# Loads of a streaming mean-subtraction kernel moved from SyncE to GpSimd, with the single-packet flag

## The chip, the cores and the metric

The kernel runs on one core of a Trainium2 chip. The metric is the device time of one execution in microseconds (us); a kernel is compared with the kernel before in alternating rounds on the same chip. Executions agree with their median within 0.3% or better (the widest range here is 1333.54 to 1338.91 us about 1336.73), and all the runs told here were in the fast state, with a granted clock of 1.0.

Some words. HBM is the chip's main memory, SBUF a core's memory on the chip, of which a tile here takes 128 partitions (rows). Sixteen DMA engines, by the profile page's count, move data between the two. A descriptor is one piece of such a transfer, here a partition's row of 33,792 B unless a run cuts it; the trace lists each as one of its "packets" (8192 of them are the 276.8 MB of the loads). The packet that the flag asks for, meant here as a group of descriptors, is not seen in the trace. Landing is the time from the issue of a transfer until its last part is reported as done. SyncE, GpSimd and the scalar engine issue transfers, each on a queue of its own (q1, q0 and q10 in the profiles); the vector engine (DVE) computes.

## The reference

```
x: (8, 4096, 2112) float32
x_r = x.reshape(B, S // 4, 4, D)
pooled = x_r.mean(axis=2)
return x - np.repeat(pooled, 4, axis=1)
```

Groups of four sequence positions lose their mean. 276.8 MB are read and as many written; nothing is used twice.

## The kernel before

A tile is 128 groups, one per partition, each with its four rows of 2112 floats side by side (33,792 B, contiguous in HBM as well). 64 tiles pass through six buffers. Cuts are marked.

```
xg = x.rearrange("b (g f) d -> (b g) (f d)", f=STRIDE)
...
io_pool = ctx.enter_context(tc.tile_pool(name="io", bufs=IO_BUFS))     # IO_BUFS = 6
sum_pool = ctx.enter_context(tc.tile_pool(name="sum", bufs=1))
for g0 in range(0, G, P):
    x_tile = io_pool.tile([P, W], mybir.dt.float32)                    # W = 4 * 2112
    nc.sync.dma_start(out=x_tile[:gsz], in_=xg[g0:g0 + gsz])           # L39: load
    ...
    # L43, L45: three adds into s;  L46: x_tile = s * (-1/4) + x_tile
    ...
    nc.scalar.dma_start(out=og[g0:g0 + gsz], in_=x_tile[:gsz])         # L54: store
```

Of the kernel before, what the change touches and what calls it, by code (L numbers as in the profile page):

```python
# [1 line left out]

# [4 lines left out]

STRIDE = 4
IO_BUFS = 6  # L10


@with_exitstack
def kernel(
    ctx: ExitStack,
    tc: tile.TileContext,
    x: bass.AP,
    out: bass.AP,
):



    nc = tc.nc
    B, S, D = x.shape
    P = nc.NUM_PARTITIONS
    assert S % STRIDE == 0
    G = (B * S) // STRIDE
    W = STRIDE * D

    xg = x.rearrange("b (g f) d -> (b g) (f d)", f=STRIDE)  # L30
    og = out.rearrange("b (g f) d -> (b g) (f d)", f=STRIDE)

    io_pool = ctx.enter_context(tc.tile_pool(name="io", bufs=IO_BUFS))
    sum_pool = ctx.enter_context(tc.tile_pool(name="sum", bufs=1))

    for g0 in range(0, G, P):
        gsz = min(P, G - g0)
        x_tile = io_pool.tile([P, W], mybir.dt.float32)
        nc.sync.dma_start(out=x_tile[:gsz], in_=xg[g0:g0 + gsz])  # L39

        rows = x_tile[:gsz].rearrange("p (f d) -> p f d", f=STRIDE)
        s = sum_pool.tile([P, D], mybir.dt.float32)
        nc.vector.tensor_add(out=s[:gsz], in0=rows[:, 0, :], in1=rows[:, 1, :])  # L43
        for f in range(2, STRIDE):
            nc.vector.tensor_add(out=s[:gsz], in0=s[:gsz], in1=rows[:, f, :])  # L45
        nc.vector.scalar_tensor_tensor(  # L46
            out=rows,
            in0=s[:gsz, None, :].to_broadcast([gsz, STRIDE, D]),
            scalar=-1.0 / STRIDE,
            in1=rows,  # L50
            op0=mybir.AluOpType.mult,
            op1=mybir.AluOpType.add,
        )
        nc.scalar.dma_start(out=og[g0:g0 + gsz], in_=x_tile[:gsz])  # L54


# [1 line left out]
_INS = ['x']  # L58
_OUTS = [((8, 4096, 2112), 'float32')]


# [23 lines left out]
```

## Time and profile before

| | before |
|---|---|
| median time | 1286.48 us (3 runs, 1286.46 to 1286.77) |
| span in the profile | 1284.7 us |
| vector engine (DVE) busy | 1026.1 us, 80% |
| DMA engines in loads / stores | 50.0% / 49.9% of 16 engines' span |
| load / store, issue to landing | 59.6 / 43.8 us (median) |

The prediction shows the lines and reads them.

### The profile page before, as it was taken

Reading aid. Unit: us, or ns where it says so; the run is one execution under the profiler, and the core shown is the slowest. Engines: PE = TensorE matmul, PEld = TensorE weight load, DVE = VectorE, ACT = ScalarE, POOL = GpSimd, SP = SyncE. Lnnn points to the kernel's source line nnn. Section 1 sums busy time; section 2 is a strip of 40 time slices with the busy share of each in tenths; the row PEclk is TensorE's granted clock in tenths of the full one; section 3 lists DMA queues with packets and bytes.
Section 4 is the critical chain, followed back from the end, with each engine's and each line's share of the span. In section 5 each row is a group of like instructions: output and inputs, shape, how many; then the busy total and the mean of one; then the engine's idle time right before and its main releaser. Section 6 shows DMA issues by size and latency. Waiting matters only on the chain.

```text
span 1284.7 us, 674 instructions
## 1 busy us (share of the span) xinstructions
DVE 1026.1 (80%) x256; POOL 0.2 (0%) x4
## 2 busy tenths in 40 slices
DVE  5998778787787877878778787787887878778784
POOL 0000000000000000000000000000000000000000
DMA  9999999999999999999999999999999999999998
GB/s 404 421 438 438 433 425 437 438 427 432 437 437 426 435 437 431 429 437 437 431 428 438 437 431 429 437 436 432 428 438 436 430 430 437 437 426 433 438 431 380
DMA packets 18437, 553.70 MB, mean 431 GB/s; under 512 B 2048, under 2 KB 2048, under 8 KB 2048
## 3 DMA queue, kind: packets, MB, share of 16 engines
q1 hardware_dynamic: 9216, 276.83, 50.0%
q10 hardware_dynamic: 9216, 276.83, 49.9%
q14 instruction: 5, 0.04, 0.0%
HBM read 276.82 MB, written 276.82 MB: 431 GB/s over the span
## 4 chain that ended last, share of the span: by engine, by line
DVE 80%; another core or an unknown queue 17%; DMA 1%; issue 1%; DVEq 0%
DVE x_tile L46 45%; DVE s L45 24%; DVE s L43 12%; DMA x_tile<-in_x_dram 1%; DVEq L43 0%
## 5 line engine op out<-in xcount | busy, mean ns | idle before, releaser
L46 DVE SCALAR_TENSOR_TENSOR x_tile<-s,x_tile 128x8448 f32<-128x8448 f32 x64 | 573.3, 8958 | 2.2
L43 DVE TENSOR_TENSOR s<-x_tile 128x2112 f32<-128x2112 f32 x64 | 150.9, 2358 | 237.5 <-DMA x_tile<-in_x_dram 237.3
L45 DVE TENSOR_TENSOR s<-s,x_tile 128x2112 f32<-128x2112 f32 x128 | 301.8, 2358 | 4.4
L69 POOL MEMSET const-bfloat16-1.0<- 128x1 bf16 x1 | 0.1, 103 | 0.0
L69 POOL MEMSET const-uint8-127<- 128x1 uint8 x1 | 0.1, 102 | 0.0
L69 POOL MEMSET const-float32-0.0<- 128x1 f32 x1 | 0.1, 100 | 0.2 <-issue 0.2
L69 POOL MEMSET const-float32-1.0<- 128x1 f32 x1 | 0.1, 99 | 0.0
## 6 DMA issues: line engine op xcount, KB each, us to landing
x_tile<-in_x_dram SPq DMA_DIRECT2D x64, 4224.0 KB, 59.6
out_dram<-x_tile ACTq DMA_DIRECT2D x64, 4224.0 KB, 43.8
```

Source lines behind the costliest of these rows:

```text
L43: nc.vector.tensor_add(out=s[:gsz], in0=rows[:, 0, :], in1=rows[:, 1, :])
L45: nc.vector.tensor_add(out=s[:gsz], in0=s[:gsz], in1=rows[:, f, :])
L46: nc.vector.scalar_tensor_tensor(out=rows, in0=s[:gsz, None, :].to_broadcast([gsz, STRIDE, D]), scalar=-1.0 / STRIDE, in1=rows, op0=mybir. ...
L69: nc = _bacc.Bacc("TRN2", target_bir_lowering=False, num_devices=1)
```

## The change

The intent is to take loads off the SyncE queue, issue them from GpSimd (the trace calls its queue software_dynamic), and ask by the flag for one packet with an engine's whole share of a tile (8 rows and one small packet of the trace, 9 descriptors: 9216 in a queue, over 64 tiles and 16 engines).

```
-        nc.sync.dma_start(out=x_tile[:gsz], in_=xg[g0:g0 + gsz])
+        nc.gpsimd.dma_start(out=x_tile[:gsz], in_=xg[g0:g0 + gsz], single_packet=True)
```

## The prediction

> **What bounds the kernel now.** The kernel streams 64 tiles of 128 rows by 33,792 bytes (four sequence positions of 2112 floats) from HBM to SBUF, works on them with the vector engine and streams them back. I read first the busy shares and the slices of the span, then the DMA queues:
>
> ```profile
> DVE 1026.1 (80%) x256; POOL 0.2 (0%) x4
> ...
> DMA  9999999999999999999999999999999999999998
> GB/s 404 421 438 438 433 425 437 438 427 432 437 437 426 435 437 431 429 437 437 431 428 438 437 431 429 437 436 432 428 438 436 430 430 437 437 426 433 438 431 380
> DMA packets 18437, 553.70 MB, mean 431 GB/s; under 512 B 2048, under 2 KB 2048, under 8 KB 2048
> ...
> q1 hardware_dynamic: 9216, 276.83, 50.0%
> q10 hardware_dynamic: 9216, 276.83, 49.9%
> ```
>
> The DMA row is 9 (90% or more) in all slices but the last, and the two queues together hold 99.9% of the time of the 16 DMA engines: 50.0% for the loads, 49.9% for the stores. Nothing is left to fill. The vector engine has 20% to spare. The same in one size: 9216 packets of a queue over 64 DMAs and 16 engines are 9 for each engine and DMA, that is 8 rows and one small packet (the 2048 under 512 B)[...]. 50.0% of 16 x 1284.7 us over 8192 data packets is 1.255 us for a packet of 33,792 B, 26.9 GB/s for an engine. 16 engines times this are 431 GB/s, the measured mean.
>
> Next, what the waits say, by groups and by DMA issue:
>
> ```profile
> L46 DVE SCALAR_TENSOR_TENSOR x_tile<-s,x_tile 128x8448 f32<-128x8448 f32 x64 | 573.3, 8958 | 2.2
> L43 DVE TENSOR_TENSOR s<-x_tile 128x2112 f32<-128x2112 f32 x64 | 150.9, 2358 | 237.5 <-DMA x_tile<-in_x_dram 237.3
> L45 DVE TENSOR_TENSOR s<-s,x_tile 128x2112 f32<-128x2112 f32 x128 | 301.8, 2358 | 4.4
> ...
> x_tile<-in_x_dram SPq DMA_DIRECT2D x64, 4224.0 KB, 59.6
> out_dram<-x_tile ACTq DMA_DIRECT2D x64, 4224.0 KB, 43.8
> ```
>
> One tile costs the vector engine 3 x 2.358 + 8.958 = 16.03 us, and it then waits about 237.3 / 59 = 4.0 us for the next load: a period of 20.0 us, which is what 2 x 8 packets of 1.255 us take on each DMA engine. The chain of waits puts 80% on the vector engine, but that is only because it follows the compute in preference to queues; it must not be read as a vector-bound kernel, since every round of it holds a wait of 4 us that a transfer ends.
>
> The buffers close the account. A buffer is 59.6 us in a load (issue to landing), 16.0 in the vector engine and 43.8 in a store: 119.4 us, six times 19.9. So of six buffers about 3 wait in the load queue, 0.8 is being worked on, 2.2 wait in the store queue. The DMA engines always have both kinds of work queued. The wait of the queue that issues the loads says the same from the other side:
>
> ```profile
> SPq L39 <- DMA out_dram<-x_tile: 1158.5, 58, 40.6
> SPq L39 <- DMA x_tile<-in_x_dram: 9.9, 1, 9.9
> ```
>
> Each load from the seventh on is released by the store that frees its buffer, 1158.5 / 58 = 20.0 us apart.
>
> [...] From the trace, (8958 - 2358) ns over (8448 - 2112) elements is 1.042 ns per element, or 0.96 elements per ns[...]. No run yet shows GpSimd beside it. [...]
>
> **The change part by part.** *Removed:* 64 load issues on SyncE, 0.33 us each, off the path. *Added:* 64 issues on GpSimd[...]. [...] even 2 us each would be 64 x 2 = 128 us of an engine that is busy 0.2 us of 1285. Their delay matters only if the DMA engines have nothing else to do meanwhile. They have: see the count of buffers. On the path lies only the first load[...]. *Kept:* bytes, rows, tile, six buffers, the order on the vector engine and the stores. The order of instructions shows one more thing: the loads now have completion semaphores of their own, so the first six are issued at once (before, the sixth waited 9.9 us for the first load to land), and each later one waits for the store that frees its buffer, as before. The sixth load sits behind five others in the queue either way: 0 us.
>
> *Moved:* the share of the engines. Before, an engine did one load row, one store row, in turn. [...] With the load landed 13 us after its buffer came free and 16 us of compute after that, the buffer joins the store queue at 29 us and has 120 - 29 = 91 us to wait and go out: store issue to landing should rise from 43.8 to about 90 us. The period must stay 20 us, because each engine still moves 16 rows of 1.255 us per tile. The buffers that queued for loads queue for stores; this moves a wait, it does not remove one.
>
> [...]
>
> *Start and end.* 64 x 16 rows x 1.255 = 1285 us is the whole span already; idle at both ends is about 2 us. At the end, loads that run early let the vector engine finish well before the stores do, so the last tens of us should be stores alone at full rate; before, the last store took 13.6 us against 10.0 of pure transfer, after the vector engine had ended. That is worth 0 to 2 us[...].
>
> Sum: 1286.5 + 1.5 (start) - 1 (end) - 1 (packets, mostly not believed) = 1286.
>
> **The rivals.** *A: software descriptors starve.* If the vector instructions lock GpSimd out, an issue waits up to 9 us for the 8.96 us instruction. [...] Even if so, the load would land after 22 us in place of 13, in a cycle of 120: the store queue still holds four tiles, 40 us of work, and the time stays. Conversely GpSimd may hold the vector engine up; with 4 us to spare in every 20, up to 4 us per tile is free. Time: 1286 to 1290. *B: the long packet[...] slow the transfer,* or one engine of the 16. As nothing is spare, this comes through in full: 3% on the loads alone is 1.5% or 19 us, 5% is 32 us and beyond the 2% mark. For: saturated engines, a path unmeasured here. Against: 9 descriptors for 270 KB in each engine are next to nothing, and load-only traffic at the start already runs at 439 GB/s from 13 to 29 us. *C: loads ahead of stores are a gain.* The vector engine's wait of 4.0 us per tile looks like a prize of 237 us. It is not: the wait follows from the transfer period, and a load landing earlier only lets its store queue earlier. [...] *D: stores starve until all six buffers await stores or compute and the engines run dry of loads.* Then they do stores, which is work that has to be done too; the engines idle only if all six buffers await the vector engine, which needs 16 us against 20. Time: unchanged.
>
> **Range and chances.** The sum gives 1286. Below, 4 to 5 us by packets and end: 1281. Above, a start of some us more or a rate lower by 0.3%: 1292. Faster by over 2% would need 440 GB/s and more[...]: 0.01. Slower by over 2% is rival B at 5% of the loads, or a serious stall that the buffers do not hide: 0.06. Within 2%: 0.93.
>
> **What the profile after would show.** Right: DMA row still 9 throughout, 431 GB/s, a load queue of software kind at about half the engines' time, vector waits of about 4 us per tile on loads, load to landing 12 to 14 us, stores about 90 us. If the landings stay at 59.6 and 43.8, packets do not set the turns as I hold. If the load queue's share of the engines rises well over 50% for the same bytes, it is rival B, and the prediction fails by half that rise. If 1285 us of DMA time stretches with slices below 9, the engines ran dry (A or D). [...]

The sum came to 1286 us; its three terms are printed, and the end (-1) rests on early loads: all three, and the 4 to 5 us that the range allows below, are guesses. The 12 to 14 us to landing held that with the flag an engine works through a load's eight rows before it turns to a store. This was an assumption that no trace had shown. The turns before the change are in the trace: from 600 us on, in stretches of 1.25 us, 11 rows of one queue start beside 5 or 6 of the other, and in the next stretch the reverse. Against rival A the trace had only the 1.042 ns an element; what that means for GpSimd was not shown yet.

## The result, and the profile after

The changed kernel took 1287.53 us in the median (5 runs, 1287.30 to 1287.59), beside 1286.77 us for the kernel before (5 runs, 1286.46 to 1286.93). The ratio is 1.0006, with a 95% interval of 0.9992 to 1.002: the same. Ratios here are the mean time of one kernel's fast runs over that of the other's fast runs of the same rounds, so they are not quite the ratio of the medians quoted. The ranges of the two kernels do not overlap, so 0.8 us may well be real, but it is 0.06%.

The page of the changed kernel, busy shares, slices and DMA queues:

```profile
DVE 1026.1 (80%) x256; POOL 34.2 (3%) x68
...
DMA  9999999999999999999999999999999999999998
...
q0 software_dynamic: 9216, 276.83, 50.0%
q10 hardware_dynamic: 9216, 276.83, 49.9%
```

The queue of the loads is now of software kind. It has the same 9216 packets and the same half of the engines' time. As before, 50.0% of 16 x 1285.8 us over 8192 data packets is 1.256 us a row: a row is neither quicker nor slower (the median row of the trace takes 1.251 us in both kernels).

The groups with waits, and the DMA issues, of the same page:

```profile
L43 DVE TENSOR_TENSOR s<-x_tile 128x2112 f32<-128x2112 f32 x64 | 151.0, 2359 | 238.4 <-DMA x_tile<-in_x_dram 238.2
L39 POOL DMA_DIRECT2D x_tile<-in_x_dram x64 | 34.0, 532 | 1161.9 <-DMA out_dram<-x_tile 1161.1
...
x_tile<-in_x_dram POOLq DMA_DIRECT2D x64, 4224.0 KB, 59.1
out_dram<-x_tile ACTq DMA_DIRECT2D x64, 4224.0 KB, 43.8
```

Three readings. GpSimd spends 532 ns on an issue, 34 us in all. The 58 issues after the first six all began and ended inside a vector instruction (56 in an add, two in the 8.96 us instruction) and took 530 ns like the others. The vector engine's wait for loads is 238.2 us, against 237.3 before. And the last two lines contradict the prediction: it expected loads to land in 12 to 14 us and stores in about 90, and they stand where they stood.

So the engines do not drain a load's eight rows in one go. The trace names no engine, but the DMA queues show this if one asks for stretches as short as one row. These are the queue lines of the changed kernel from 600 to 601.25 us, and then from 601.25 to 602.5 us (packets that start there, MB, share of 16 engines):

```profile
q0 software_dynamic: 15, 0.51, 93.8%
q10 hardware_dynamic: 1, 0.03, 6.3%
```
```profile
q10 hardware_dynamic: 15, 0.51, 93.8%
q0 software_dynamic: 1, 0.03, 6.3%
```

In one row's time 15 of the 16 engines start a load row, in the next 15 start a store row; the two stretches after repeat this. With turns of a whole load, load rows would have filled eight such stretches in a row. With this flag set, the engines change queues after every descriptor of 33,792 B. An assignment of the packets to engines by start and end finds the same in the whole middle of the run (190 to 990 us): all but two of 5117 load turns are one row long.

Where do the 0.8 us come from? The timeline from the start, first of the kernel before, then of the changed one (start, duration, engine, line, operation, and in brackets the idle time before):

```profile
0.73 12.64 SPq L39 DMA_DIRECT2D x_tile<-in_x_dram  x6
13.05 2.36 DVE L43 TENSOR_TENSOR s<-x_tile 128x2112 f32<-128x2112 f32 x1 [13.05 <-DMA x_tile<-in_x_dram]
```
```profile
1.25 3.27 POOL L39 DMA_DIRECT2D x_tile<-in_x_dram  x6 [0.81 <-PEq L80]
13.89 2.36 DVE L43 TENSOR_TENSOR s<-x_tile 128x2112 f32<-128x2112 f32 x1 [13.89 <-DMA x_tile<-in_x_dram]
```

SyncE issued its first load at 0.73 us, GpSimd at 1.25. The first load then takes 12.32 us to reach the vector engine from SyncE, 12.64 from GpSimd. Together this is 0.84 us. The last vector instruction starts 0.93 us later than before (1262.23 against 1261.30) and the span is 1.1 us longer, so the start travels through to the end of a pipeline without slack. What counts is when the DMA engines begin, not the vector engine: the first data packet of the trace starts at 1.74 us before and at 2.62 us after, and the last one ends 0.95 us later (1284.51 against 1283.56 us). Two runs below start the vector engine some 7 and 12 us later than the changed kernel and lose far less than that.

### The profile page after: what moved, and what is told of

It reads as the page before. It is cut to its first block, busy times and chain, and to the rows that moved or that the text cites. A ratio compares the mean times of both kernels' runs of the same rounds, so it can differ in the third digit from the quotient of the medians.

```text
span 1285.8 us, 676 instructions
## 1 busy us (share of the span) xinstructions
DVE 1026.1 (80%) x256; POOL 34.2 (3%) x68
## 3 DMA queue, kind: packets, MB, share of 16 engines
q0 software_dynamic: 9216, 276.83, 50.0%
q10 hardware_dynamic: 9216, 276.83, 49.9%
## 4 chain that ended last, share of the span: by engine, by line
DVE 80%; another core or an unknown queue 17%; DMA 1%; issue 1%; DVEq 0%; PEldq 0%
DVE x_tile L46 45%; DVE s L45 24%; DVE s L43 12%; DMA x_tile<-in_x_dram 1%; DVEq L43 0%; PEldq L80 0%
## 5 line engine op out<-in xcount | busy, mean ns | idle before, releaser
L46 DVE SCALAR_TENSOR_TENSOR x_tile<-s,x_tile 128x8448 f32<-128x8448 f32 x64 | 573.3, 8958 | 2.2
L43 DVE TENSOR_TENSOR s<-x_tile 128x2112 f32<-128x2112 f32 x64 | 151.0, 2359 | 238.4 <-DMA x_tile<-in_x_dram 238.2
L39 POOL DMA_DIRECT2D x_tile<-in_x_dram x64 | 34.0, 532 | 1161.9 <-DMA out_dram<-x_tile 1161.1
## 6 DMA issues: line engine op xcount, KB each, us to landing
x_tile<-in_x_dram POOLq DMA_DIRECT2D x64, 4224.0 KB, 59.1
out_dram<-x_tile ACTq DMA_DIRECT2D x64, 4224.0 KB, 43.8
```

What stands on the lines that cost most here:

```text
L39: nc.gpsimd.dma_start(out=x_tile[:gsz], in_=xg[g0:g0 + gsz], single_packet=True)
L43: nc.vector.tensor_add(out=s[:gsz], in0=rows[:, 0, :], in1=rows[:, 1, :])
L46: nc.vector.scalar_tensor_tensor(out=rows, in0=s[:gsz, None, :].to_broadcast([gsz, STRIDE, D]), scalar=-1.0 / STRIDE, in1=rows, op0=mybir. ...
```

## The experiments

The questions are these. Does the flag do anything, and what sets the engines' turns (theory D: every descriptor; rivals: the packet, or bytes)? The letters B, C, D, G and P in the expectations are explained there and are not the prediction's rivals of the same letter; A and A' go back to its rival A. Does giving loads a larger share gain anything? Is the start the cost? Would a GpSimd that is held up have been hidden? Each run gives its median beside the median of the kernel before on the same chip.

**The flag alone.**

```
-        nc.gpsimd.dma_start(out=x_tile[:gsz], in_=xg[g0:g0 + gsz], single_packet=True)
+        nc.gpsimd.dma_start(out=x_tile[:gsz], in_=xg[g0:g0 + gsz])
```

> The changed kernel without the single-packet flag, loads still from GpSimd. Theory D (an engine changes queue after every descriptor, so the flag cannot move shares): landings stay near 59.1 us for loads and 43.8 us for stores, 1251 ns per row packet, time 1287.5 within 0.5 us. Rival P (the flag does set the turn, but something else holds the landings): landings or GpSimd's 532 ns per issue change visibly. Rival C (the flag costs or saves time that offsets the start): the time moves by 1 us or more.

1287.46 us beside 1286.54 (ratio 1.0007, 0.9994 to 1.0021), landings 59.1 and 43.8 us, 532 ns an issue. Without the flag the kernel is the same in every number within the noise: no effect of the flag is seen here, and the 0.8 us belong to the move to GpSimd. (The first vector instruction came at 14.05 us here and at 13.89 with the flag, with the issue at 1.25 us in both: the start is known to some 0.2 us.)

**Loads in small descriptors, with the flag and without.**

```
-                            single_packet=True)
+                            single_packet=True, max_dma_last_dim=5632)
```

> Changed kernel with each load row cut in six descriptors of 5632 B[...]; stores keep 33792 B. Theory D (turn after each descriptor): while both queues have work a load gets 5632 of 39424 bytes, 1/7, so stores rush: store landing about 13 to 16 us, load landing about 120 - 16 - 15 = 89 us. Rival P (turn after the packet of 48): loads rush, landing 12 to 15 us, stores near 90. Rival B (turns by bytes): 59 and 44 stay. Time in all: 1287.5 if a descriptor costs nothing of its own[...].

1319.65 us beside 1286.54 (ratio 1.0256, 1.0242 to 1.027). The DMA issues of this run:

```profile
x_tile<-in_x_dram POOLq DMA_DIRECT2D x64, 4224.0 KB, 89.1
out_dram<-x_tile ACTq DMA_DIRECT2D x64, 4224.0 KB, 16.0
```

A load now hands the engine over after 5632 B and a store after 33,792 B, so stores overtake. The order of the packets shows the turns themselves: by the same assignment to engines, a store row is followed by one small load piece in 4316 of 4961 cases in the middle of the run; the rest are mostly long runs of load pieces (22 to 82), which fits a store queue that is empty once a store has landed (16.0 us of a period of 20). Theory D said 89 and 13 to 16; turns by packet would have given the reverse, turns by bytes no change. The time rose by 33 us. The load queue now has 51.0% of 1317.8 us for an engine, 672 us, in place of 50.0% of 1285.8, 643 us: 29 us for 5 x 512 more descriptors in an engine. (A piece takes 0.218 us, six of them 1.31 us, in place of 1.251 for a row.) The end costs too, since the stores no longer have a queue to work on while the last tiles load and are computed. The windows of the end:

```profile
1290.00:1300.00 10.00, 9.90 (x4) 0.00 (x0) 1.00 0.60 260
1300.00:1310.00 10.00, 5.51 (x1) 0.00 (x0) 1.00 0.38 162
```

The last two columns are DMA share and GB/s: some 10 us of idle engines in 20. The two terms add up to more than the 32 us by which the spans differ, because the packets' times in the trace overlap by some 8 us an engine more than in the changed kernel.

> Loads from GpSimd in six descriptors a row, without the single-packet flag. With it the run of small loads measured 89.1 us and 16.0 us to landing and 1319.65 us. Theory D (turns by descriptor, flag of no effect on turns): the same landings within 1 us, time 1317 to 1322. Rival (packets do play a part with several descriptors in a default packet, or the flag saves descriptor cost): landings or time move by more than that.

The same without `single_packet=True`: 1318.79 us (1318.31 to 1319.11) beside 1286.54, in place of 1319.65 (1317.24 to 1321.26).

```profile
x_tile<-in_x_dram POOLq DMA_DIRECT2D x64, 4224.0 KB, 89.0
out_dram<-x_tile ACTq DMA_DIRECT2D x64, 4224.0 KB, 16.0
```

Even with 49 descriptors in an engine's share, the flag changes neither turns nor time.

> The same small descriptors, loads from SyncE. Theory D: the turn is taken by descriptor on the hardware path as well, landings near 89 and 16 us, and the cost of 6 times as many descriptors is again about 33 us over 1286.5. Rival[...]: time clearly under 1319, say 1290 to 1305.

The same small loads from SyncE: 1317.26 us beside 1286.54 (ratio 1.0237), stores 16.0 us. The rival put the cost of small descriptors down to GpSimd's path. They cost 30.7 us from SyncE and 33.1 from GpSimd, so for the most part it is not that. Loads landed in 68.5 us, not 89: SyncE itself waited before most issues (875.9 us in 51 waits put down to the vector engine), so part of a buffer's wait lay ahead of the issue. That part of the expectation was wrong and was not followed further.

**Stores in small descriptors.**

```
-        nc.scalar.dma_start(out=og[g0:g0 + gsz], in_=x_tile[:gsz])
+        nc.scalar.dma_start(out=og[g0:g0 + gsz], in_=x_tile[:gsz], max_dma_last_dim=5632)
```

> Changed kernel with the stores' rows cut in six descriptors of 5632 B and the loads left at 33792 B. Theory D: a load gets 6/7 while both have work, so load landing falls to 13 to 16 us and store landing rises to about 89 us: the shift that the prediction expected of the flag, now by descriptor size; the time must then stay at 1287.5[...], with no gain from the early loads. Rival P or B: 59 and 44 stay. Rival G (early loads are a gain): clearly under 1287.

1336.73 us beside 1286.54 (ratio 1.0388, 1.0374 to 1.0402). Landings 18.8 and 77.1 us (13 to 16 and about 89 were expected): in kind the shift that had been predicted of the packet, now by descriptor size. The price was 50 us. The stores' queue took 50.6% of 1334.5 us (675 us against 642) and the loads' 49.3% (658 against 643): 33 and 15 us. Their sum is the difference of the spans within a microsecond, but partly by luck: the engines are also idle 6.5 us longer at the end, and the packets' times overlap by about as much more. Why whole-row loads are slowed as well is open. The run shows turns, but with this price it cannot show what early loads are worth; the next one can.

**A larger share for loads, nothing cut.**

```
+        if (g0 // P) % 2:
+            nc.sync.dma_start(out=x_tile[:gsz], in_=xg[g0:g0 + gsz])
+        else:
             nc.gpsimd.dma_start(out=x_tile[:gsz], in_=xg[g0:g0 + gsz], single_packet=True)
```

> Loads in turn from SyncE and GpSimd, all descriptors whole rows: three queues with one row each in turn, so loads together get up to 2/3. No descriptor is cut. Theory D (turn after each descriptor, and a share only moves the wait): load landing falls from 59 to about 30 us, store landing rises from 44 to about 74 us (120 - 16 - 30), the time stays at 1287 within 1.5 us. Rival G (loads ahead of stores are a gain): under 1283. Rival (issuing engine does not matter to the shares): 59 and 44 stay.

1288.58 us beside 1286.53 (ratio 1.0016, 1.0002 to 1.0029). The issues:

```profile
out_dram<-x_tile ACTq DMA_DIRECT2D x64, 4224.0 KB, 77.3
x_tile<-in_x_dram SPq DMA_DIRECT2D x32, 4224.0 KB, 24.9
x_tile<-in_x_dram POOLq DMA_DIRECT2D x32, 4224.0 KB, 25.7
```

With loads on two queues and stores on a third, loads land in 25 us and stores in 77 (some 30 and 74 were expected). The sum with the 16.03 us of vector work is 118.6 us, the same six periods as before (119.4). The wait moved by 34 us per tile, and the time did not fall: it rose by 2 us, a little more than the 1.5 allowed. At the start two loads share the engines, and the first vector instruction starts only at 26.3 us; but the engines are busy meanwhile, and their idle time at both ends is no longer than in the changed kernel. The 2 us lie in the rows: those that start between 30 and 100 us take up to 2.59 us in place of 1.251, 1.8 us an engine more than in the changed kernel. Why is open. Rival C of the prediction, that early loads are a gain, is out.

**The start.**

```
+        if g0 == 0:                                  # second run: g0 < IO_BUFS * P
+            nc.sync.dma_start(out=x_tile[:gsz], in_=xg[g0:g0 + gsz])
+        else:
             nc.gpsimd.dma_start(out=x_tile[:gsz], in_=xg[g0:g0 + gsz], single_packet=True)
```

> The changed kernel with only the first tile's load issued from SyncE. Theory (the added 0.8 us of the median is the later start of the first load: first vector instruction at 13.89 us against 13.05 before): the first vector instruction is back at about 13.05 us and the span at 1284.7 to 1285.0, 0.8 us below the changed kernel. Rival (the software queue is slower by 0.06% all along): span stays at 1285.5 to 1285.8.

A miss: 1287.19 us beside 1286.54, span 1285.9. The single SyncE load shared the engines with GpSimd's queue and landed after 20.0 us, so the first vector instruction came at 20.76 us, not 13.05. Its first data packet did start as early as before (1.74 us), and the median is still 0.65 us up; in its profile rows between 30 and 50 us took 0.4 us an engine longer than before, and the rest is open. The run changes more than the start and separates nothing; it does show that 7.7 us at the first vector instruction do not cost 7.7 us.

> The changed kernel with the first six loads (one round of buffers) from SyncE and the other 58 from GpSimd, so that one queue alone is loading at the start, which the run with a single SyncE load did not give (two queues shared the engines, the first load landed at 20.0 us). Theory (start): the first transfer runs in the second microsecond of the span as before (share over 1 there, 0 in the changed kernel), the first vector instruction starts at 13.05 us within 0.2, and the span is 1284.7 to 1285.0, the median 0.8 us under the changed kernel's. Rival (the software path costs along the way or at the end): span stays at 1285.6 to 1285.9 although the start is early.

1286.76 us (1286.67 to 1286.93) beside 1286.53 (1286.40 to 1286.94). The first microseconds by DMA share and GB/s (last two columns), of the changed kernel and of this run:

```profile
1.00:2.00 1.00, 0.00 (x0) 0.75 (x2) 1.00 0.00 0
2.00:3.00 1.00, 0.00 (x0) 1.00 (x3) 1.00 1.37 406
```
```profile
1.00:2.00 1.00, 0.00 (x0) 0.00 (x0) 1.00 1.43 406
2.00:3.00 1.00, 0.00 (x0) 0.00 (x0) 1.00 0.41 135
```

The transfers start a microsecond earlier, and the median stands 0.23 us over the kernel before in place of 0.76 (the changed kernel) and 0.92 (without the flag). With 58 of 64 loads still in software, most of the difference thus goes with the first six loads, and the first data packet (1.73 us) is where it was before: the start, by this one run. The expectation was a little high: the first vector instruction came at 13.27 us and the span was 1285.2. The last 0.2 us are within the noise of the two ranges.

This run has a second use. Its landings are 24.8 us (GpSimd's loads) and 78.1 us (stores), with the same two queues in the steady state as in the changed kernel. Turns are equal in both (most load turns are one row long here too, the rest two), so landings alone do not prove a share: with equal turns, whatever split of six buffers between the two queues the first round leaves can stay. That the start set it is an inference; that the split is worth nothing is measured once more.

**A late issue.**

```
+        if g0 >= IO_BUFS * P:
+            nc.gpsimd.memset(x_tile[:gsz], 0.0)
         nc.gpsimd.dma_start(out=x_tile[:gsz], in_=xg[g0:g0 + gsz], single_packet=True)
```

> The changed kernel with a GpSimd fill of the whole tile ahead of each load from the seventh on; the fill waits for the buffer as the load did, so each load is issued later by its duration (to be read from the run; the scheduler puts two fills before two loads, so every second load is later by another period). It stands for a GpSimd that is held up, the doubled wait of rival A. Theory (a late issue is hidden while the load queue holds about three loads, 60 us of landing of which 20 are needed): landing falls by the delay, time within 3 us of 1287.5. Rival A in its strong form (issue time is on the path): at least 58 x 5 = 290 us more.

1287.84 us beside 1286.53 (ratio 1.001). The fill took 7.14 us; the scheduler put two ahead of two loads, so one load in two was held back by 7 us, the other by 27. Landing fell from 59.1 to 42.7 us, and the vector engine's wait is 238.2 us, unchanged. A delay of this size is hidden, as the prediction held.

**A vector instruction of twice the rate** (wrong results on purpose).

```
-        (the three adds and the scalar_tensor_tensor)
+        for f in range(3):                           # later runs: range(4)
+            nc.vector.tensor_scalar(out=x_tile[:gsz], in0=x_tile[:gsz], scalar1=1.0,
+                                    scalar2=None, op0=mybir.AluOpType.mult)
```

> Wrong result on purpose: the vector engine runs three single-input fp32 multiplications by one over the whole 128x8448 tile instead of its four instructions, to see whether a vector mode[...] (about 4.5 us each if it is taken, 8.9 if not) holds up GpSimd's descriptor writing. If it does: GpSimd's issue grows from 532 ns to microseconds in part of the 64 cases, up to 4.5 us. If not: it stays at 532 ns. The time must in either case stay at 1287 within 3 us, if the vector work is under 20 us per tile; at 3 x 8.9 = 26.7 us per tile the vector engine becomes the bound, near 64 x 26.9 = 1720 us, and the run tells nothing on the mode.

1289.74 us beside 1286.53. An instruction took 4556 ns for 8448 elements, 0.54 ns each, about half of the 1.06 ns that the kernel's 8958 ns instruction takes. "Two-element" stands for this rate below. All issues but one took about 0.53 us; none of them overlapped a vector instruction, since they fell into the 6.4 us in which the vector engine waited for a load. The one of 2.38 us began at 52.89 us and ended at 55.27; the vector engine was busy without a break from 14.09 to 55.15. The extra 2 us lie in the end: the DMA share was 0.54 from 1260 to 1270 us.

> Wrong result on purpose: as the run with three two-element multiplications (4.556 us each; there GpSimd's issues fell into the 6.4 us in which the vector engine waited and took 527 ns, all but one of 2.38 us), but with four, 18.2 us of every 20, so that most issues must meet a busy vector engine. Theory A' (this vector mode keeps GpSimd from writing descriptors until the instruction ends, and the kernel's own instructions do not): issues of 1 to 5 us in most of the 58 later loads, in place of 532 ns. Rival: they stay at 527 to 532 ns and the one of 2.38 us was something else. On the time both theories agree: the delay is hidden by the queues, so 1287 to 1295 with a longer end (the last tile's vector work is 4.6 us longer than with three); if the delay were on the path, 58 x 2 us = 116 us more.

1394.17 us beside 1286.49 (ratio 1.0838, 1.082 to 1.0856). The groups of this run, and below them the timeline from 440 to 620 us:

```profile
L43 DVE TENSOR_SCALAR x_tile<-x_tile 128x8448 f32<-128x8448 f32 x256 | 1145.5, 4557 | 234.4 <-DMA x_tile<-in_x_dram 234.3
L39 POOL DMA_DIRECT2D x_tile<-in_x_dram x64 | 640.3, 10010 | 663.7 <-DMA out_dram<-x_tile 662.9
```
```profile
458.87 85.00 DVE L43 TENSOR_SCALAR x_tile<-x_tile 128x8448 f32<-128x8448 f32 x19 [18.32 <-DMA x_tile<-in_x_dram]
...
493.82 51.72 POOL L39 DMA_DIRECT2D x_tile<-in_x_dram  x4 [41.39 <-DMA out_dram<-x_tile]
```

Twelve of the 64 issues, counted in the timeline, took 49.8 to 52.2 us; their sum is what makes 640.3. In the case shown, the first of the four took 50.17 us, to 543.99 us. The vector engine ran 19 instructions without a break until 458.87 + 85.00 = 543.87. They start 4.47 us apart and last 4.56, so none leaves a gap. All twelve ended 0.12 us after such an unbroken run of 19 to 22 instructions did, eleven of which had begun after the issue; the other 52 issues overlapped no vector instruction. GpSimd is shut out not for one instruction but until the vector engine runs dry of loads, which GpSimd's own lateness brings about. My expectation had the wait right and its length wrong (1 to 5 us per issue). A wait of 50 us outlasts the queues: the DMA mean fell from 431 to 398 GB/s.

> Wrong result on purpose: the four two-element vector instructions of the run at 1394.17 us, with the loads issued from SyncE and all else equal. Theory A' (twelve of GpSimd's issues lasted about 51 us because the vector engine left no gap, and only the software path can be locked out): no such wait, the transfers bind again with 18.2 us of vector work in every 20, time 1287 to 1295 (a longer end than before). Rival (the vector engine at 18.2 us per tile with six buffers is itself the cause of the 8%): again above 1380.

The same vector work with SyncE loads took 1286.05 us beside 1286.68 (ratio 0.9994, 0.9978 to 1.0011). This is a little under the 1287 to 1295 expected. So 18.2 us of vector work per tile is not the cause; GpSimd's issue beside those instructions is. Nor is it enough that the vector engine is busy: in the run with the first six loads from SyncE, 54 of GpSimd's 58 issues fell into the 8.96 us instruction of one element in 1.06 ns, and took 530 to 664 ns.

## Why the prediction was right or wrong

The time (1286.0, range 1281 to 1292) and the class were right, and the ground for them was right: the DMA engines are full (99.9% of their time in both kernels), and a row costs the same whoever issues it (1.255 us from SyncE, 1.256 from GpSimd). The sum was not tested by this: its terms (+1.5, -1, -1, all guesses) made the change 0.5 us faster, and it came out 0.76 us slower, both far inside the range. The steps:

- *Bound by the 16 DMA engines at 20.0 us a tile*: held. Loads at 50.0% and stores at 49.9% of the engines' time, 431 GB/s, vector wait 238.2 us.
- *"Moved": a load as one packet of eight rows, landing in 12 to 14 us, stores at about 90*: wrong. This is the step that failed: loads landed in 59.1 us and stores in 43.8, the very sign that the prediction named for it ("packets do not set the turns as I hold"). The engines take turns by descriptor, as the alternating stretches, the small loads (89.1 and 16.0 us) and the flag's lack of any effect show. The equal shares of 50.0 and 49.9% before the change could not tell: equal bytes at equal time a row give equal shares under any turns. The prediction's inference, that such a shift would move a wait and not the time, was tested with another means (two load queues, 25 and 77 us) and held.
- *Start, +1.5 us*: it measured +0.84 us at the first vector instruction, of which 0.52 is the later issue and some 0.3 the slower way to the first packet and landing; putting the first six loads back on SyncE removed most of it.
- *End, -1 us*: 0. It rested on early loads. It would not have come anyway: with early loads (first six from SyncE) the span was 1285.2 us. The opposite shift does cost, as the idle engines at the end of the small-load run show.
- *Packets, -1 us*: 0 (the ground for a gain was not from a trace). A row still takes 1.256 us. (The 439 GB/s that the prediction read for the loads at the start is no higher rate: that window has a DMA share of 1.02, as it counts packets by their start.)
- *Rival A, starving software descriptors*: absent in this kernel. The issues took 532 ns, while vector instructions ran, and the vector engine was busy for 1026.1 us as before. It was underrated, though: "up to 9 us" and "the time stays" hold only for an engine that leaves gaps. With two-element instructions and few gaps, the wait was 50 us and the time rose by 8.4%.
- *Rival B, a slower transfer*: not seen; loads take 50.0% of the engines' time, as from SyncE. (More descriptors do cost: 2560 more for an engine took 29 us in the small-load run, some 11 ns each.) *Rival D*: never arose.

Open: whether the flag reaches the DMA engines at all, whether descriptors this large (5632 B and up were tried) each end a packet in spite of it, or whether the engines disregard packet borders when they change queues. All three give what was measured.

## What to carry to other kernels

When the DMA engines are full, ask three things of a change to the issuing side: does it alter the engines' time per byte, does it delay the first transfer, and does it anywhere leave the engines without work (at the end, or while an issue is held up)? A share that moves between loads and stores moves a wait (34 us per tile with two load queues, and the time rose by 2 us); here descriptor size moved it (landings of 89.1 and 16.0 us with small loads), and the packet flag did not (89.0 and 16.0 without it). Before loads go to GpSimd, look at the vector instructions: at 1.06 to 1.12 ns an element they left its issues alone (532 ns), at 0.54 ns and without gaps they shut it out for 50 us at a time. A neutral result at full queues is thus no licence for the same change elsewhere.
